# Five split-weight buffers at five byte offsets, and three matmul orders in the up projection

## The chip, the cores and the metric

The kernel runs on one core of one Trainium2 chip. The metric is device time in microseconds (us) for one execution of the whole program. The engines are named as in the profile: PE (TensorE, matmuls), PEld (its weight loads), DVE (VectorE), ACT (ScalarE), POOL (GpSimd) and SP (SyncE, which issues most DMAs). In a matmul, one operand is stationary (a 128 x 128 weight load ahead of the matmul) and the other is streamed through (up to 512 columns).

## The reference

One encoder block on 256 tokens with 2048 features, in float32. Cut to what matters here:

```
hn = rmsnorm(h, mix_norm_pre);  proj = hn @ w_in       # stages dtu, xbc, z
y  = [bidirectional SSD mixer, pooling mixer];  h += rmsnorm(y @ w_out)   # stage wo
hn = rmsnorm(h, ffn_norm_pre)
up = hn @ w_up                                          # stage up: 2048 x 11264
gate, val = split(up, 2)
ff = (gelu(dwconv(gate)) * val) @ w_down                # stage down (dn): 5632 x 2048
h += rmsnorm(ff)
gate = sigmoid(rmsnorm(h) @ w_gate)                     # stage gt
h += rmsnorm(gate * (p @ w_ple))                        # stage ple
```

## The kernel before

All large products are made at better than single-pass precision by splitting each operand into a high part (rounded to float32r) and a low part (the rest), and adding high x high, high x low and low x high. Weights come from HBM in float32 into one of three `raw` buffers. `split` (L142) then makes the two halves: ACT casts the high half (L154), DVE subtracts it from the raw weights to get the low half (L155). The halves lie in two tiles of 1056 float32r per partition, with the tags `whi` and `wlo`, of five buffers each, used in rotation. Each buffer has 4224 bytes in each partition. In the allocation of the program the five `whi` buffers, in the order in which they are used, start at bytes 42848, 59744, 55520, 51296 and 47072 of the partition, and the `wlo` buffers at 63968, 80864, 76640, 72416 and 68192. After them come 13 pages of 8192 bytes, from byte 85088 on, which hold activations and much else. Raw buffers lie ahead of the split buffers.

The kernel goes through its stages in the order of the reference. In all of them except xbc and up, activations are the stationary operand and the split weights are streamed. In xbc and up it is the other way round.

Up is the largest stage. Its output of 11264 features is cut into 11 slabs of 512 for the gate and 11 for the value, and each slab into two halves of 256 features (`i`), so that there are 44 blocks. A block takes 16 k-tiles of 128 input features; four k-tiles make a weight piece (128 x 1024), so that there are 176 pieces (`NPIECES`). `feature_pairs` (L384) issues the 16 matmuls of a piece: for each of four k-tiles and each of two groups of 128 features, the high half against a high-and-low pair of activations side by side (512 columns, `get.both(k)`), and then the low half against the high activations (256 columns), added onto the second half of the same accumulator:

```
mm(acc[f], wh[:, s], get.both(k), k == 0, False)
mm(acc[f][:, L:], wl[:, s], get(k)[0], False, k == NK - 1)
```

All matmuls are issued by the helper `mm`, so that the profile lists them under L90. The activations of up are in four pages (`wox`), with 2048 bytes for each k-tile. The main loop splits five pieces ahead (`next_part`), and after each piece one more, which is the piece five later. At the end of a block, `total` (L396) adds the two halves of each accumulator: ACT copies one (L399), DVE adds the other (L400). A pair of accumulators belongs to a block, and there are six such tiles, three pairs.

The order of ACT, DVE and SP in up is that in which the program lists the work (`in_order`). PE takes its matmuls in the order of the program.

In the names of the profile, numbers are left out: `ug_0h` is the high half of an even gate piece, `uv_1l` the low half of an odd value piece, `ga` and `va` the accumulators of gate and value, `dn...` those and the weights of down.

Of the kernel before, what the change touches and what calls it, by code (L numbers as in the profile page):

```python
# [12 lines left out]
F32R = mybir.dt.float32r  # L13
# [4 lines left out]
P = 128  # L18
L = 256
D = 2048  # L20
NK = D // P
# [32 lines left out]
def build(nc, a, out):  # L54
    x = a["x"][0]
# [5 lines left out]
    with tile.TileContext(nc) as tc, \  # L61
# [9 lines left out]
        def ins(r):  # L71
            return getattr(r, "ins", r)

        def page(name, dtype=F32):
            return gp.tile([P, 2048], dtype, tag="pg", bufs=13, name=name)
# [7 lines left out]
        def main(name):  # L83
            return [pm.tile([P, 512], F32, tag="main", name=f"{name}_{i}") for i in range(2)]
# [4 lines left out]
        def mm(o, lhsT, rhs, start, stop):  # L89
            last["pe"] = ins(nc.tensor.matmul(o, lhsT, rhs, start=start, stop=stop, skip_group_check=True))  # L90
# [15 lines left out]
        acc, acc2 = [main(f"dtu{t}") for t in range(2)], main("dtu2")  # L106
# [27 lines left out]
        low, among, four = small[:64, 592:593], small[:64, 593:597], small[:64, 597:601]  # L134
# [4 lines left out]

        spare, ready = {}, {}  # L140

        def split(name, src, nel, cuts=()):  # L142

            if name in ready:
                return ready.pop(name)
            if name in spare:
                hi, lo = spare.pop(name)
            else:
                hi = wp.tile([P, 1056], F32R, tag="whi", bufs=5, name=f"{name}h")
                lo = wp.tile([P, 1056], F32R, tag="wlo", bufs=5, name=f"{name}l")  # L150
            for c0, c1 in zip((0, *cuts), (*cuts, nel)):
                s = slice(c0, c1)
                if (name, c0) != ("dtu0", 0):
                    last["act"] = ins(nc.scalar.copy(hi[:, s], src[:, s]))  # L154
                last["dve"] = ins(nc.vector.tensor_sub(lo[:, s], src[:, s], hi[:, s].bitcast(F32)))  # L155
            return hi, lo
# [44 lines left out]
        @contextmanager  # L201
        def in_order():


            block = nc.cur_bb.bb.instructions
            seen = {i.name for i in block}
            yield
            for i in block:
                if i.name in seen or i.engine not in ORDERED:
                    continue  # L210
                if i.engine in chain:
                    tc.add_manual_dep(i, chain[i.engine].name,
                                      mybir.DependencyInfo(mybir.DependencyClass.NoSync, mybir.DependencyReason.DATA),
                                      reason="in_order")
                chain[i.engine] = i
# [58 lines left out]
        def seven_products(name, stage, w, k0, c0, a_, acc, alt, start, stop):  # L274

            if (stage, c0, k0) in sums_:
                r = raw(f"{name}r")
                last["dma"] = load(r[:, 512:], w[c0 // 1024, k0 // 2][:, 512:], not name.startswith(IN_ORDER))  # L280
                t, held = sums_[stage, c0, k0]
                if not held:
                    t = lp.tile([P, 2048], F32, tag="own", bufs=1, name=f"{name}t") if name == "gt18" else page(f"{name}t")
                    last["dma"] = load(t, sums_[stage, c0, k0][0], not name.startswith((*IN_ORDER, "gt18")))
            else:
                r = t = raw(f"{name}r", w[c0 // 1024, k0 // 2])
                if stage in APART:
                    t = page(f"{name}t")
                    add_blocks(r, t)
            b11 = split(f"{name}a", r[:, 512:1024], 512)  # L290
            b2 = split(f"{name}b", r[:, 1024:], 1024)
            if r is t:
                add_blocks(r)
            t42 = split(f"{name}d", t[:, 1024:], 1024)
            t31 = split(f"{name}c", t[:, :1024], 1024)

            for x, (wh, wl), c, o, own in (
                    ("a11", b11, 0, alt[0], True), ("a12", b2, 0, acc[0][0], False), ("a22", t42, 0, acc[1][0], False),
                    ("s4", b2, 512, acc[0][1], False), ("s2", t42, 512, alt[3], True), ("s1", t31, 512, alt[1], True),
                    ("s3", t31, 0, alt[2], True)):  # L300
                xh, xl = a_[x]
                for q, (xx, ww) in enumerate(((xh, wh), (xh, wl), (xl, wh))):
                    mm(o, xx, ww[:, c:c + 512], own and start and q == 0, own and stop and q == 2)
# [77 lines left out]
                                   k == 0 and q == 0 and f % 2 == 0, k == NK - 1 and q == 2)  # L381
                aside()

        def feature_pairs(n, part, get, acc):  # L384

            wh, wl = part
            for kk in range(4):
                k = 4 * n + kk  # L390
                for f in range(2):
                    s = slice(kk * 256 + f * P, kk * 256 + (f + 1) * P)
                    mm(acc[f], wh[:, s], get.both(k), k == 0, False)
                    mm(acc[f][:, L:], wl[:, s], get(k)[0], False, k == NK - 1)

        def total(o, acc):  # L396

# [79 lines left out]
                done = put(hn(k), x_part(k), vec(V_MIX + k))  # L477
            return done

        spare["dtu0"] = [wp.tile([P, 1056], F32R, tag=f"w{c}", bufs=5, name=f"dtu0{c[0]}") for c in ("hi", "lo")]  # L480
        turned = ins(nc.vector.tensor_copy(spare["dtu0"][0][:, :352], r0[:, :352]))
        with tc.issue_after(turned):
            front = x_panel(0, 1)
# [2 lines left out]
        for u in range(0, NK, 2):  # L486
            r = [wp.tile([P, 2048], F32, tag="raw", bufs=3, name=f"dtur{u}") if u else r0, page(f"dtur{u + 1}")]
            for j in range(2):
                k = u + j
# [17 lines left out]
            for j in range(2):  # L507
                k = u + j
                with tc.issue_after(front[0]), tc.issue_after(front[1]):
                    wh, wl = split(f"dtu{k}", r[j][:, :1056], 1056, ((352, 704), (704,), (352,))[k] if k < 3 else ())  # L510
# [234 lines left out]
        def job(f, *args):  # L745
            return lambda: f(*args)
# [83 lines left out]
        def gload(name, src):  # L830
            g = cp.tile([P, D], F32, tag="gain", name=name)
            load(g, src.partition_broadcast(P))
            return g
# [90 lines left out]
        h = [page(f"h{t}") for t in range(2)]  # L924
        for t in range(2):
            load(h[t], x[t * P:(t + 1) * P, :])
        hf = sublayer("wo", w_out, (list(range(8, 16)) + list(range(8)), [8,9,10,11,12,13,0,1,2,3,14,15,4,5,6,7]), cat, gload("gmix", a["mix_norm_post"][0]), h,
                      V_FN, Pairs, ((4,5),(2,3,4)), Sums("cs", cat))
# [42 lines left out]
        for i, w_ in enumerate(which[2:] + which[:2]):  # L971
            fetch, add, store = block_sums(*w_, i >= len(which) - 2)
            n = 45 * i // 10 + 4
# [62 lines left out]
        parts, slab = [], {}  # L1036

        def next_part():

            n = len(parts)  # L1040
            if n < NPIECES:
                s, v, i = blocks[n // 4]
                name = f"u{'gv'[v]}{s}{i}"
                if n % 2 == 0:
                    slab["raw"] = raw(f"{name}r{n // 2 % 2}", w_up[v, s, i, n // 2 % 2])
                parts.append(split(f"{name}{n // 2 % 2}_{n % 2}", slab["raw"][:, n % 2 * 1024:(n % 2 + 1) * 1024], 1024))
# [9 lines left out]
        def gate_norm(s, i):  # L1056
            v = slab[s][0][:, i * 512:(i + 1) * 512].rearrange("p (f t) -> p f t", f=2)
            nc.vector.tensor_tensor(v, v, slab["rfb"].unsqueeze(1).to_broadcast([P, 2, L]), op=ALU.mult)  # L1058
# [25 lines left out]
        with in_order():  # L1084
            for _ in range(5):
                next_part()
            for n in range(NPIECES):
                s, v, i = blocks[n // 4]
                if n % 4 == 0:
                    acc = main(f"{'gv'[v]}a{s}{i}")  # L1090
                with tc.issue_after(last["pe"]) if n in (6, 8) else nullcontext():
                    feature_pairs(n % 4, parts[n], hf, acc)
                if n % 4 == 3:
                    (value_out if v else gate_out)(s, i, acc)

                if n == 3:
                    row[0]()
                elif n == 5:
                    row[1]()
                next_part()  # L1100
                if n == 5:
                    row[2]()
                    gate_norm(0, 0)
                elif n in (6, 7):
                    (gelu if n == 7 else gate_conv)(0, 0)
                elif n >= 8 and n % 4 < 2 and blocks[n // 4 - 1][1] == 0:
                    (gelu if n % 4 else gate_conv)(blocks[n // 4 - 1][0], blocks[n // 4 - 1][2])
                for job in jobs_at[n]:
                    job()
# [114 lines left out]
        for half in range(2):  # L1224

            alt = [] if half else main(f"gts{half}")
            acc = [main(f"gt{half}{t}") for t in range(2)]
# [13 lines left out]
            for t in range(2):  # L1241
                for n, (o, c0) in enumerate(columns(acc[t])):
                    c1 = c0 + o.shape[-1]
                    c = slice(half * 1024 + c0, half * 1024 + c1)
# [102 lines left out]
```

## Time and profile before

| | |
|---|---|
| runs | 1109.44, 1109.47, 1108.57 us (median 1109.44) |
| span of the profiled execution, first to last instruction | 1106.4 us |
| its own time beside the span | not listed; the median lies 3.0 us above the span |
| granted TensorE clock, mean | 0.997 |
| PE busy | 1098.2 us, 99% |
| DVE busy | 978.2 us, 88% |
| ACT busy | 729.5 us, 66% |
| mean DMA rate | 327 GB/s |
| up on PE | from 289.1 to 783.9 us |

The busy time of PE counts each matmul from its start until its modelled end, and matmuls overlap in the pipeline (a 512-column matmul is listed with 0.39 us, but the next one starts after 0.23). So the pace of PE is read from one start to the next, and not from busy times.

### The profile page before, as it was taken

How to read it: one execution, taken by the hardware profiler on the slowest of the kernel's cores; microseconds unless marked ns; L12 is line 12 of the kernel's file. 1: busy time of each engine (PE TensorE's matmuls, PEld its weight loads, DVE VectorE, ACT ScalarE, POOL GpSimd, SP SyncE). 2: the span in 40 equal slices, each digit the busy share in tenths (PEclk: the TensorE clock that was granted, in tenths of full speed). 3: DMA queues.
4: the chain of work that ended last, by engine and by line, in shares of the span. 5: the costliest groups of instructions: out<-in, count | busy, mean ns of one | idle time of the engine just before them, and what ended most of it. 6: DMA issues, size and time to landing. Idle time of an engine off the chain costs nothing.

```text
span 1106.4 us, 16113 instructions
## 1 busy us (share of the span) xinstructions
PE 1098.2 (99%) x5946; PEld 947.8 (86%) x5946; DVE 978.2 (88%) x1372; ACT 729.5 (66%) x1067; POOL 86.2 (8%) x145
## 2 busy tenths in 40 slices
PE   9999999999999999999999999999999999999997
PEld 9999988888888888888888888888888888888886
DVE  6589998898868998889889988888999999999996
ACT  6958763556775565565756646657688878777773
POOL 0200000100100000000000000000000000051001
PEclk9999999999999999999999999999999999999998
DMA  9985358556589999989999998999999999995872
GB/s 366 364 336 187 111 191 346 209 211 231 182 356 400 400 403 349 394 350 367 386 359 373 369 394 335 405 356 421 357 408 370 376 346 388 414 384 220 315 270 76
DMA packets 57247, 361.71 MB, mean 327 GB/s; under 512 B 6352, under 2 KB 7504, under 8 KB 21200
## 3 DMA queue, kind: packets, MB, share of 16 engines
q1 hardware_dynamic: 45648, 298.71, 69.4%
q0 software_dynamic: 11088, 61.35, 14.4%
q8 instruction: 47, 0.77, 0.3%
q10 hardware_dynamic: 432, 0.62, 0.2%
q14 instruction: 32, 0.26, 0.1%
HBM read 306.65 MB, written 54.00 MB: 326 GB/s over the span
## 4 chain that ended last, share of the span: by engine, by line
PE 97%; ACT 1%; DVE 1%; issue 0%; POOL 0%; POOLq 0%
PE ga L90 22%; PE va L90 22%; PE dna L90 11%; PE woa L90 6%; PE xbc L90 5%; PE gt L90 5%; PE dns L90 4%; PE dtu L90 4%; PE z L90 4%; PE dn0s L90 2%; PE dn1s L90 2%; PE ple L90 1%; PE gts L90 1%; PE yd L90 1%; PE wos L90 1%; PE pw L90 1%
## 5 line engine op out<-in xcount | busy, mean ns | idle before, releaser
L90 PE MATMUL ga<-wox,ug_0h 128*128 128x512 f32 x352 | 125.5, 395 | 0.0
L90 PE MATMUL ga<-wox,ug_1h 128*128 128x512 f32 x352 | 125.2, 394 | 0.0
L90 PE MATMUL va<-wox,uv_0h 128*128 128x512 f32 x352 | 124.8, 393 | 0.0
L90 PE MATMUL va<-wox,uv_1h 128*128 128x512 f32 x352 | 124.8, 393 | 0.0
L90 PE MATMUL ga<-wox,ug_1l 128*128 128x256 f32 x352 | 99.1, 282 | 0.0
L90 PE MATMUL va<-wox,uv_0l 128*128 128x256 f32 x352 | 99.1, 281 | 0.0
L90 PE MATMUL va<-wox,uv_1l 128*128 128x256 f32 x352 | 99.1, 281 | 0.0
L90 PE MATMUL ga<-wox,ug_0l 128*128 128x256 f32 x352 | 99.1, 281 | 0.0
L272 DVE TENSOR_TENSOR dnb<-dnb 128x512 f32<-128x512 f32 x128 | 88.3, 690 | 3.0
L90 PEld LDWEIGHTS va<-wox,uv_0h 128*128 128x128 f32 x352 | 66.1, 188 | 15.0
L90 PEld LDWEIGHTS ga<-wox,ug_1h 128*128 128x128 f32 x352 | 66.1, 188 | 15.0
L90 PEld LDWEIGHTS va<-wox,uv_1h 128*128 128x128 f32 x352 | 66.1, 188 | 15.0
L90 PEld LDWEIGHTS ga<-wox,ug_0h 128*128 128x128 f32 x352 | 66.1, 188 | 14.8
L90 PEld LDWEIGHTS ga<-wox,ug_0l 128*128 128x128 f32 x352 | 66.2, 188 | 0.1
L90 PEld LDWEIGHTS ga<-wox,ug_1l 128*128 128x128 f32 x352 | 66.2, 188 | 0.0
L90 PEld LDWEIGHTS va<-wox,uv_0l 128*128 128x128 f32 x352 | 66.2, 188 | 0.0
L90 PEld LDWEIGHTS va<-wox,uv_1l 128*128 128x128 f32 x352 | 66.2, 188 | 0.0
L247 POOL DMA_DIRECT2D dns<-dnb x30 | 16.1, 536 | 321.8 <-DVE dnb L272 281.0
L843 ACT CAST he<-he 128x512 fp32r<-128x512 f32 x13 | 8.1, 621 | 41.9 <-DVE he L842 41.9
L985 ACT CAST hs<-hid 128x384 fp32r<-128x384 f32 (+1 forms) x44 | 23.4, 536 | 13.6 <-PE dna L90 13.3
L1065 ACT ACTIVATE fc<-gr,vt 128x256 f32<-128x256 f32 x44 | 26.1, 593 | 6.2 <-DVE gr L1058 6.1
L1136 POOL DMA_DIRECT2D hd<-hsum x24 | 12.9, 539 | 193.4 <-PE dn0s L90 83.1
(2491 smaller groups left out, 3300.4 us busy)
## 6 DMA issues: line engine op xcount, KB each, us to landing
dnb<-w_down SPq DMA_DIRECT2D x32, 1024.0 KB, 10.3
dns<-dnb POOLq DMA_DIRECT2D x30, 1024.0 KB, 6.8
hd<-hsum POOLq DMA_DIRECT2D x24, 512.0 KB, 8.3
zr<-w_z SPq DMA_DIRECT2D x8, 1024.0 KB, 4.9
dtur<-w_dtu SPq DMA_DIRECT2D x14, 528.0 KB, 8.5
hsum<-he POOLq DMA_DIRECT2D x13, 512.0 KB, 7.6
wo0r<-w_out_ SPq DMA_DIRECT2D x6, 1024.0 KB, 7.0
gtb<-w_gate SPq DMA_DIRECT2D x6, 1024.0 KB, 10.0
```

The source lines that it names most:

```text
L90: last["pe"] = ins(nc.tensor.matmul(o, lhsT, rhs, start=start, stop=stop, skip_group_check=True))
L247: nc.gpsimd.dma_start(t, pg[0])
L272: nc.vector.tensor_add(s[:, i], v[:, i], a[:, b])
L843: nc.scalar.copy(o[:, :512], s[:, :512])
L985: nc.scalar.copy(t[:, :c1], hid_part(k)[:, :c1])
L1065: nc.scalar.activation(c[:, f], v[:, f], AF.Identity, bias=vec(V_FCB + 4 * s + 2 * i + f), scale=vec(w + NF))
L1136: nc.gpsimd.dma_start(o.bitcast(F32), kept[k])
```

## The change

Instead of a `whi` and a `wlo` tile, each piece takes one tile which holds both halves, with a tag of its own for each of the five places in the rotation. The list `PLACES` gives each tile's size and where in it the high and the low half begin, in float32 elements. With the same start of the weights area as before, tiles laid out in the order of first use would begin at bytes 42848, 51424, 60000, 68608 and 77088, and the pages behind them at 85568. The halves then begin at these bytes modulo 256:

| place | 0 | 1 | 2 | 3 | 4 |
|---|---|---|---|---|---|
| high half, before | 96 | 96 | 224 | 96 | 224 |
| low half, before | 224 | 224 | 96 | 224 | 96 |
| high half, after | 96 | 224 | 0 | 32 | 64 |
| low half, after | 96 | 224 | 128 | 160 | 192 |
| pages, before / after | 96 / 64 | | | | |

In up, `feature_pairs` gets an order, which is the slab's number modulo 3: 0 is the order of before (one high, one low), 1 is two high and then two low, 2 is all eight high and then all eight low.

```diff
+        PLACES = ((2144, 0, 1088), (2144, 0, 1088), (2152, 40, 1096), (2120, 8, 1064), (2120, 8, 1064))
+        rotation = [0, 1, 2, 3, 4]
+
+        def weight_pair(name):
+            n = rotation.pop(0)
+            rotation.append(n)
+            size, h0, l0 = PLACES[n]
+            w = wp.tile([P, size], F32R, tag=f"w{n}", bufs=1, name=f"{name}w")
+            return w[:, h0:h0 + 1056], w[:, l0:l0 + 1056]
+
         def split(name, src, nel, cuts=()):
...
-                hi = wp.tile([P, 1056], F32R, tag="whi", bufs=5, name=f"{name}h")
-                lo = wp.tile([P, 1056], F32R, tag="wlo", bufs=5, name=f"{name}l")
+                hi, lo = weight_pair(name)
...
-        def feature_pairs(n, part, get, acc):
+        def feature_pairs(n, part, get, acc, order):
             wh, wl = part
-            for kk in range(4):
+
+            def high(kk, f):
                 k = 4 * n + kk
-                for f in range(2):
-                    s = slice(kk * 256 + f * P, kk * 256 + (f + 1) * P)
-                    mm(acc[f], wh[:, s], get.both(k), k == 0, False)
-                    mm(acc[f][:, L:], wl[:, s], get(k)[0], False, k == NK - 1)
+                mm(acc[f], wh[:, kk * 256 + f * P:kk * 256 + (f + 1) * P], get.both(k), k == 0, False)
+
+            def low(kk, f):
+                k = 4 * n + kk
+                mm(acc[f][:, L:], wl[:, kk * 256 + f * P:kk * 256 + (f + 1) * P], get(k)[0], False, k == NK - 1)
+
+            every = [(kk, f) for kk in range(4) for f in range(2)]
+            groups = ([(x,) for x in every], [every[i:i + 2] for i in range(0, 8, 2)], [every])[order]
+            for g in groups:
+                for x in g:
+                    high(*x)
+                for x in g:
+                    low(*x)
...
-        spare["dtu0"] = [wp.tile([P, 1056], F32R, tag=f"w{c}", bufs=5, name=f"dtu0{c[0]}") for c in ("hi", "lo")]
+        spare["dtu0"] = weight_pair("dtu0")
...
-                    feature_pairs(n % 4, parts[n], hf, acc)
+                    feature_pairs(n % 4, parts[n], hf, acc, s % 3)
```

## The prediction

> **What bounds the kernel now.** I read the page first (busy shares, the chain that ended last), then the time that PE spent waiting, then two stretches of the order of time on PE, down to single starts.
>
> ```profile
> PE 1098.2 (99%) x5946; PEld 947.8 (86%) x5946; DVE 978.2 (88%) x1372; ACT 729.5 (66%) x1067; POOL 86.2 (8%) x145
> ...
> PEclk9999999999999999999999999999999999999998
> ...
> PE 97%; ACT 1%; DVE 1%; issue 0%; POOL 0%; POOLq 0%
> PE ga L90 22%; PE va L90 22%; PE dna L90 11%; PE woa L90 6%; PE xbc L90 5%; PE gt L90 5%; PE dns L90 4%; PE dtu L90 4%; PE z L90 4%; PE dn0s L90 2%; PE dn1s L90 2%; PE ple L90 1%; PE gts L90 1%; PE yd L90 1%; PE wos L90 1%; PE pw L90 1%
> ```
>
> 97% of the chain is PE, at full granted clock; 44% of it is up (`ga`, `va`). What PE waited for in the whole span, and up against the neighbouring stretch:
>
> ```profile
> PE gof L90 <- ACT godg L1209: 1.9, 1, 1.9
> PE dtu L109 <- POOL ident masks.py:199: 1.4, 1, 1.4
> PE seg L90 <- ACT E L633: 0.2, 1, 0.2
> ```
>
> ```profile
> 289.10:783.90 494.80, 494.80 (x2846) 434.43 (x2846) 433.00 (x614) 303.64 (x460) 28.19 (x54) 1.00 0.95 370
> 784.00:1008.00 224.00, 224.00 (x975) 181.71 (x973) 214.26 (x255) 175.15 (x224) 30.52 (x33) 1.00 0.94 369
> ```
>
> PE waits 3.5 us in 1106.4 us, and none of it in up. So only the spacing of matmuls, start to start, can change the time; what ACT and DVE do matters only if they fall so far behind that PE starts to wait. Here are single starts in up. A weight piece is 16 matmuls, eight on the high half (512 columns) and eight on the low half (256); the rows kept are those at the start of six pieces, with two pairs inside the first.
>
> ```profile
> 451.50 0.39 PE L90 MATMUL va<-wox,uv_1h 128*128 128x512 f32 x1
> 451.72 0.28 PE L90 MATMUL va<-wox,uv_1l 128*128 128x256 f32 x1
> 451.84 0.40 PE L90 MATMUL va<-wox,uv_1h 128*128 128x512 f32 x1
> 452.08 0.28 PE L90 MATMUL va<-wox,uv_1l 128*128 128x256 f32 x1
> 452.20 0.40 PE L90 MATMUL va<-wox,uv_1h 128*128 128x512 f32 x1
> ...
> 454.31 0.39 PE L90 MATMUL va<-wox,uv_0h 128*128 128x512 f32 x1
> ...
> 457.09 0.39 PE L90 MATMUL va<-wox,uv_1h 128*128 128x512 f32 x1
> ...
> 459.90 0.39 PE L90 MATMUL va<-wox,uv_0h 128*128 128x512 f32 x1
> ...
> 462.68 0.39 PE L90 MATMUL va<-wox,uv_1h 128*128 128x512 f32 x1
> ...
> 465.46 0.39 PE L90 MATMUL va<-wox,uv_0h 128*128 128x512 f32 x1
> ```
>
> The pieces last 2.81, 2.78, 2.81, 2.78 and 2.78 us, 13.96 us for one turn through the five buffers: 2.792 on average (176 of them are 491.4 of the stage's 494.8 us). Nothing waits here, and the work is the same in all five; what differs is the buffer. In the program's allocation before, a 13-slot page of activations always starts at 96 mod 256, and the buffers of 4224 bytes alternate: in order of use the high half lies at 96, 96, 224, 96, 224 and the low half 128 bytes away from it. The two slow pieces are the two with the high half at 224. So address does count here, by 0.03 us or 1% of a piece. Measured from the page, the fast kind has its high half at 0 and its low half at 128, the slow kind 128 and 0.
>
> **The change, part by part.**
>
> *New offsets from the page.* The five new tiles take 480 bytes more than the ten old ones, so that the pages behind them move to 64 mod 256. Laid out in the order of first use, the pairs lie at (96, 96), (224, 224), (0, 128), (32, 160), (64, 192); from the page that is (32, 32), (160, 160), (192, 64), (224, 96), (0, 128). One of five is the fast kind of before. The other four use six offsets that up has not shown; the two known ones give 2.78 and 2.81, and I take their middle, 2.795, for each. A turn is then (2.78 + 4 x 2.795) / 5 = 2.792 us a piece: no change. The nearest rows for other offsets are in ple, where the stationary operand (`pth`, `ptl`, at 64) and the streamed buffers (96 and 224) are 96 or 224 apart, beside the same kind of matmul in down, where they are 0 or 128 apart:
>
> ```profile
> 283.87 0.39 PE L90 MATMUL ple<-ple_1h,ptl 128*128 128x512 f32 x1
> ...
> 285.48 0.39 PE L90 MATMUL ple<-ple_0h,pth 128*128 128x512 f32 x1
> ...
> 850.16 0.39 PE L90 MATMUL dn0s<-dn026dh,hd 128*128 128x512 f32 x1
> 850.38 0.39 PE L90 MATMUL dn0s<-dn026dl,hd 128*128 128x512 f32 x1
> 850.61 0.40 PE L90 MATMUL dn0s<-dn026dh,hd 128*128 128x512 f32 x1
> 850.85 0.39 PE L90 MATMUL dns<-dn026ch,hd 128*128 128x512 f32 x1
> ...
> 856.37 0.40 PE L90 MATMUL dn0s<-dn028ch,hd 128*128 128x512 f32 x1
> ```
>
> In ple there are 7 spacings in 1.61 us, 0.230 each; in down 27 in 6.21 us, 0.230 each. Single ones swing between 0.22 and 0.24 in down, and are steady in ple, but the mean is the same at both sets of offsets. This is my reason for the middle, and for 0 in all other stages, where the split buffers are streamed: 1,918 matmuls of 512 columns there. Bounds: in up, worst is every new pair at the longest pair above (451.84 to 452.20, 0.36), 2.88 a piece, (2.78 + 4 x 2.88) / 5 - 2.792 = 0.068, times 176 = +12.0 us; best is the shortest (451.50 to 451.84, 0.34), 2.72 a piece, -0.060 x 176 = -10.6 us. For the 1,918 others all at 0.22 or all at 0.24 would be 19 us either way; since the swing averages out in both rows, I keep 0.002 of it, 4 us either way.
>
> *Three orders.* Slabs 0, 3, 6, 9 keep high, low, high, low: 64 pieces. Slabs 1, 4, 7, 10 take two high, two low, and slabs 2, 5, 8 eight high, eight low: 112 pieces. The count of matmuls, weight loads and columns is the same; only neighbours change, from 512 beside 256 to 512 beside 512 and 256 beside 256. The first kind of run is down's 0.230. The second is xbc's, whose 24 rows from the first to the last of these hold 23 spacings:
>
> ```profile
> 60.64 0.28 PE L90 MATMUL xbc<-hnh,xb_1h 128*128 128x256 f32 x1
> ...
> 63.36 0.28 PE L90 MATMUL xbc<-hnh,xb_1l 128*128 128x256 f32 x1
> ```
>
> 2.72 / 23 = 0.1183 us. Eight of each are 8 x (0.230 + 0.1183) = 2.786 us, against 2.792 on average now: -0.006 x 112 = -0.7 us. Bounds: all of these pieces as the fast or the slow kind, -0.012 or +0.018 a piece, -1.3 or +2.0 us; this lies inside the bounds above.
>
> *One tile for both halves.* A buffer now comes free when both halves have been read. In up the last matmul of a piece is a low one in every order, so ACT's cast of a high half may start one low spacing, 0.12 us, later than before. Who feels it:
>
> ```profile
> 451.57 1.05 ACT L154 CAST uv_1h<-uv31r 128x1024 fp32r<-128x1024 f32 x1 [1.33 <-PE va L90]
> ```
>
> This cast starts when the piece before 451.50 has ended, and fills the buffer of the piece that starts at 462.68: 11.1 us of cover for 1.05 us on ACT and the subtraction on DVE behind it. Price 0. Queued behind that cast on ACT are the copies and convolution of the gate, with the same cover. In the other stages that split five at a time the high half is read last or one matmul apart, so the joint release comes with the high half's own: 0. In the first stage (dtu) the low product may follow by up to six matmuls; four pieces lie between: 0.
>
> *Reading out.* `total` reads f = 0 first. Its last matmul is now the last but one of a block in seven slabs (0.12 us before the end instead of 0.35), so ACT's copy starts 0.23 us later, 28 times. The accumulators are three deep (six tiles, two a block), so PE needs them again two blocks, or 22 us, later: 0. No DMA, queue or instruction is added; SP and POOL are not touched.
>
> **Sum:** 0 - 0.7 + 0 + 0 = -0.7 us. The profiled execution has a span of 1106.4 us, so 1105.7 after; the median of the runs shown, 1109.44, lies 3.0 us above the span, which I carry over: 1108.7 us.
>
> [...]
>
> **Rivals.**
>
> *Slower: the new offsets lock in the slow rhythm.* Place: the four new pairs in up, in any order. For it: a slow kind exists, holds through a whole piece, and the present layout has it in only two of five; single pairs reach 0.36. Against it: ple's offsets cost nothing. Price: all four at 2.81 is (2.78 + 4 x 2.81) / 5 - 2.792 = 0.012 x 176 = +2.1 us; at 2.88 it is +12.0. It decides when the four average over about 2.81. I put its middle at 1115 us.
>
> *Faster: the new offsets or the grouping avoid stalls.* For it: 0.34 and 0.22 occur, so neither 0.348 nor 0.230 is a floor. Against it: they never occur twice running. Price: all at the fast kind -2.1 us, at 2.72 -10.6; middle 1104 us.
>
> *The shared tile makes PE wait.* If a matmul on a high half had to wait for the DVE's write of the low half in the same tile, the price is up to about 1 us (the cast above takes 1.05) wherever a split is used at once; the first piece of dtu and a few units of down (DVE 214.26 of 224.00 us busy) are such places: +2 to +5 us, 1112 us. Against it: the low half is needed one matmul later anyway.
>
> **How the numbers follow.** About 2.2 us (0.2%) is what a measurement of this kernel can tell from no change. No change within that, around 1108.7: 0.44. Slower by offsets 0.25, by the shared tile 0.04: 0.29 together. Faster: 0.27. The time is that of the likeliest case, whose own range is 1107.2 to 1111.6. The full range takes in most of both rivals: half of the bounds of up below (-5.3) and two thirds above (+8.0): 1103 to 1117.
>
> **What would show it.** Right: pieces in up between 2.77 and 2.82 us in every order and buffer, PE still without a wait there, 512-column spacing in down at 0.230. Wrong: one offset whose pieces leave that band by several per cent, a slab order with its own level, a new line of PE waits on ACT or DVE, or a stage outside up that changes its spacing because its streamed buffers moved.

## The result and the profile after

The changed kernel took 1113.23 us (median of three, 1113.20 to 1114.55) against 1109.44 before: a ratio of 1.0042, with a 95% interval of 1.0027 to 1.0057. The ratio is estimated from all executions; the two medians alone give 1.0034. The kernel is slower by 0.4%, where 1108.7 and "no change" was forecast. The profiled execution took 1114.55 us, with a span of 1111.6 against 1106.4.

Busy times and chain, and what PE waited for (total in us, times, longest), from the page and the waits of the changed kernel:

```profile
PE 1103.6 (99%) x5946; PEld 948.7 (85%) x5946; DVE 978.7 (88%) x1372; ACT 728.8 (66%) x1067; POOL 84.2 (8%) x145
...
PE 97%; ACT 1%; DVE 1%; issue 0%; POOL 0%; POOLq 0%
```

```profile
PE gof L90 <- ACT godg L1226: 1.9, 1, 1.9
PE dtu L109 <- POOL ident masks.py:199: 1.4, 1, 1.4
PE seg L90 <- ACT E L650: 0.2, 1, 0.2
```

No wait has come, and none has grown: PE issues the same 5946 matmuls, and takes 5.2 us longer. So they stand further apart. By their starts, the last of which comes 5.4 us later, 1.6 us lie in up, 3.0 in the other stages from z on, and 0.8 ahead of z, where the profiles of the next five kernels also have 0.2 to 0.5 us more than before, those with the spacing of before included. Two stretches, one inside up and one inside down, count the matmuls. In these rows the first number behind the stretch is its length, the next are PE's busy time and its matmuls, then PEld, DVE, ACT, POOL, the granted clock, the DMA share and GB/s. First before, then after:

```profile
340.00:760.00 420.00, 420.00 (x2408) 368.63 (x2408) 369.45 (x522) 251.32 (x375) 24.45 (x46) 1.00 0.96 377
800.00:1000.00 200.00, 200.00 (x868) 162.35 (x867) 193.11 (x228) 158.06 (x198) 26.00 (x23) 1.00 0.96 379
```

```profile
340.00:760.00 420.00, 420.00 (x2402) 367.13 (x2401) 368.15 (x519) 247.41 (x372) 24.46 (x46) 1.00 0.96 375
800.00:1000.00 200.00, 200.00 (x862) 161.58 (x861) 191.86 (x226) 161.14 (x201) 26.33 (x24) 1.00 0.96 379
```

At the same clock, 6 matmuls fewer in 420 us of up (0.2%) and 6 fewer in 200 us of down (0.7%). Down loses more, though only up was given new orders. From the starts of all matmuls with 512 columns in both traces (outside up, two such in a row, without 28 that exceed 270 ns and one of 28 ns): 230.7 ns before and 232.3 after, 1,869 pairs in each; times 1,918 matmuls, this is 3.2 us. The table sorts them by offset: the byte address of the weights loaded meanwhile minus that of the operand that is streamed, modulo 256. The weights loaded meanwhile are those of the next matmul: in the kernel before, the load for the matmul at 850.38 us starts at 850.16, as the matmul ahead of it does; a load takes 188 ns. The changed kernel has these means:

| offset | 0 | 32 | 64 | 96 | 128 | 160 | 192 | 224 |
|---|---|---|---|---|---|---|---|---|
| ns, after | 230.8 | 233.3 | 232.0 | 234.1 | 232.1 | 233.5 | 230.6 | 231.6 |
| ns, before | 230.6 | | | | 230.7 | | | |

In up the order of time shows one row for a piece, since both halves have one name now. A place is the position of a piece's buffer in the rotation of five. These are pieces of a slab with the order of before (places 4, 0, 1, 2), of one with two and two (places 0, 1, 2), and of one with eight and eight (places 1, 2, 3); the start is the first number:

```profile
431.26 2.94 PE L90 MATMUL ga<-wox,ug_1w 128*128 128x512 f32 x16
434.04 2.94 PE L90 MATMUL ga<-wox,ug_0w 128*128 128x512 f32 x16
436.81 2.97 PE L90 MATMUL ga<-wox,ug_1w 128*128 128x512 f32 x16
439.62 2.87 PE L90 MATMUL ga<-wox,ug_0w 128*128 128x512 f32 x15
...
475.94 2.98 PE L90 MATMUL ga<-wox,ug_1w 128*128 128x512 f32 x16
478.75 2.98 PE L90 MATMUL ga<-wox,ug_0w 128*128 128x512 f32 x16
481.57 2.98 PE L90 MATMUL ga<-wox,ug_1w 128*128 128x512 f32 x16
...
520.84 2.99 PE L90 MATMUL ga<-wox,ug_1w 128*128 128x512 f32 x16
523.67 2.93 PE L90 MATMUL ga<-wox,ug_0w 128*128 128x512 f32 x16
526.44 2.96 PE L90 MATMUL ga<-wox,ug_1w 128*128 128x512 f32 x16
```

From one start to the next: 2.78, 2.77, 2.81 us, then 2.81 and 2.82, then 2.83 and 2.77. The medians over all pieces, in ns, by order (one high and one low in turn, two and two, eight and eight) and place:

| order, offsets (high, low) from the page | (32, 32) | (160, 160) | (192, 64) | (224, 96) | (0, 128) | mean |
|---|---|---|---|---|---|---|
| one, one | 2776 | 2807 | 2826 | 2774 | 2778 | 2792 |
| two, two | 2814 | 2822 | 2813 | 2777 | 2807 | 2807 |
| eight, eight | 2812 | 2832 | 2765 | 2801 | 2790 | 2800 |

Before, in the one order, the five places have 2775, 2776, 2816, 2777, 2816, which is 2792 on average. So up grew by 64 x 15 + 48 x 8 ns = 1.3 us by its orders. In the old order the new offsets leave the average where it was, 2792, though no longer each piece. (From the first to the last start the stage took 1.6 us more; the rest is in its first pieces.)

### The profile page after: what moved, and what is told of

Read it like the earlier page. It is cut to its first block, busy times and chain, and to the rows that moved or that the text cites. A ratio compares the mean times of both kernels' runs of the same rounds, so it can differ in the third digit from the quotient of the medians.

```text
span 1111.6 us, 16016 instructions
## 1 busy us (share of the span) xinstructions
PE 1103.6 (99%) x5946; PEld 948.7 (85%) x5946; DVE 978.7 (88%) x1372; ACT 728.8 (66%) x1067; POOL 84.2 (8%) x145
## 4 chain that ended last, share of the span: by engine, by line
PE 97%; ACT 1%; DVE 1%; issue 0%; POOL 0%; POOLq 0%
PE ga L90 22%; PE va L90 22%; PE dna L90 11%; PE woa L90 6%; PE xbc L90 5%; PE gt L90 5%; PE dns L90 4%; PE dtu L90 4%; PE z L90 4%; PE dn0s L90 2%; PE dn1s L90 2%; PE ple L90 1%; PE gts L90 1%; PE wos L90 1%; PE yd L90 1%; PE pw L90 1%
## 5 line engine op out<-in xcount | busy, mean ns | idle before, releaser
L90 PE MATMUL ga<-wox,ug_0w 128*128 128x512 f32 (+1 forms) x704 | 132.0, 338 | 0.0
L90 PE MATMUL ga<-wox,ug_1w 128*128 128x512 f32 (+1 forms) x704 | 131.3, 338 | 0.0
L90 PE MATMUL va<-wox,uv_1w 128*128 128x512 f32 (+1 forms) x704 | 130.4, 337 | 0.0
L90 PE MATMUL va<-wox,uv_0w 128*128 128x512 f32 (+1 forms) x704 | 130.3, 337 | 0.0
L90 PEld LDWEIGHTS ga<-wox,ug_0w 128*128 128x128 f32 x704 | 109.8, 188 | 15.6 <-ACT pl L933 0.2
L90 PEld LDWEIGHTS ga<-wox,ug_1w 128*128 128x128 f32 x704 | 109.7, 188 | 15.5
L90 PEld LDWEIGHTS va<-wox,uv_1w 128*128 128x128 f32 x704 | 109.7, 188 | 15.5
L90 PEld LDWEIGHTS va<-wox,uv_0w 128*128 128x128 f32 x704 | 109.7, 188 | 15.5
L90 PE MATMUL xbc<-hnh,xb_0w 128*128 128x256 f32 x192 | 37.7, 283 | 0.0
L90 PE MATMUL xbc<-hnh,xb_1w 128*128 128x256 f32 x192 | 37.1, 282 | 0.0
```

## The experiments

Every kernel was timed beside the kernel before; ratios are to it, with 95% intervals. Offsets are modulo 256.

### The parts alone

Only the places (the call in up passes order 0):

```diff
-                    feature_pairs(n % 4, parts[n], hf, acc, s % 3)
+                    feature_pairs(n % 4, parts[n], hf, acc, 0)
```

> The five new places, with the order of before (high, low, high, low) in all slabs of up. Theory A (the streamed buffers' offsets from the page cost time outside up, and the grouping costs time in up): in the changed kernel the slabs that kept this order averaged 2792 ns a piece, as before, so up stays within 0.5 us; outside up 512-column matmuls stay at 232.3 ns against 230.7 before, 1,918 of them: +3.2 us, about 1112.6. Theory B (the grouping alone is the cause): 1109.4. Theory C (the tile shared by both halves makes someone wait): about 1113, with the loss in waits and not in spacing.

Measured 1111.79 against 1108.53 us, ratio 1.0029 (1.0017 to 1.0040). Its rows for the two stretches:

```profile
340.00:760.00 420.00, 420.00 (x2409) 367.56 (x2408) 369.53 (x521) 250.18 (x374) 24.47 (x46) 1.00 0.96 377
800.00:1000.00 200.00, 200.00 (x862) 161.53 (x861) 191.63 (x226) 159.33 (x199) 26.40 (x24) 1.00 0.96 379
```

Up is back at 2409 matmuls; down has the 862 of the changed kernel. So the offsets cost 3.3 us (1111.79 - 1108.53), and all but 0.2 of it outside up.

Only the orders (the ten tiles of before, `whi` and `wlo`):

```diff
-            w = wp.tile([P, size], F32R, tag=f"w{n}", bufs=1, name=f"{name}w")
-            return w[:, h0:h0 + 1056], w[:, l0:l0 + 1056]
+            hi = wp.tile([P, 1056], F32R, tag="whi", bufs=5, name=f"{name}h")
+            lo = wp.tile([P, 1056], F32R, tag="wlo", bufs=5, name=f"{name}l")
+            return hi, lo
```

> The ten buffers of before, with three orders by slab. Theory A: outside up nothing changes (230.7 ns); in up the grouped slabs rise from 2792 to about 2800 to 2807 ns a piece (the averages of these slabs in the changed kernel), 112 pieces: +0.9 to +1.7 us, 1110.3 to 1111.1. Theory B: the whole loss, about 1113. Theory C: 1109.4.

Measured 1111.07 us, ratio 1.0022 (1.0013 to 1.0032).

```profile
340.00:760.00 420.00, 420.00 (x2400) 368.17 (x2399) 368.22 (x520) 248.66 (x374) 24.46 (x46) 1.00 0.96 375
800.00:1000.00 200.00, 199.94 (x865) 161.48 (x864) 192.53 (x227) 159.05 (x200) 17.77 (x24) 1.00 0.97 381
```

Up loses 8 matmuls in 420 us: its grouped slabs average 2805 (two and two) and 2808 (eight and eight), 64 x 13 + 48 x 16 ns = 1.6 us. Spacing outside up is as before, 230.7 ns. The profiled execution has 0.9 us more in down, in eight late starts. These are not spacing: weight loads waited there for DVE, 0.2 to 0.5 us each, the first of them for a low half that DVE had only just written:

```profile
860.30 0.19 PEld L90 LDWEIGHTS dna<-dn030bl,hs 128*128 128x128 f32 x1 [0.46 <-DVE dn030bl L159]
```

The changed kernel has no such wait in this part of down; a later kernel, the one that takes its lead-in from the map, has 0.9 us of late starts there too. Whether the orders brought these waits about is not shown. Both parts cost, and theory B, the orders alone, has fallen.

One tile, old offsets and order:

```diff
-        PLACES = ((2144, 0, 1088), (2144, 0, 1088), (2152, 40, 1096), (2120, 8, 1064), (2120, 8, 1064))
+        PLACES = ((2112, 0, 1056), (2112, 0, 1056), (2112, 1056, 0), (2112, 0, 1056), (2112, 1056, 0))
```

> One tile for both halves as in the changed kernel, but the halves at the offsets of before (high at 96, 96, 224, 96, 224, low 128 away, pages at 96), and the order of before. Theory A: spacing as before everywhere, pieces of 2776 and 2816 ns in the same rhythm, 1109.4. Theory B: 1109.4. Theory C: about 1113, with new waits of PE or ACT.

Measured 1108.54 us, ratio 1.0002 (0.9993 to 1.0011), with PE's three waits as they were. The pieces in up have the levels of before to 1 ns. Sharing a tile costs nothing that shows; theory C has fallen. With 3.3 us for the places and 1.3 for the orders, 4.6 us are accounted for; from the 1108.53 of 20 executions of the kernel before to 1113.23 it is 4.7.

### Is it the offset?

The kernel before with 32 bytes more between buffers and pages:

```diff
         spare["dtu0"] = [wp.tile([P, 1056], F32R, tag=f"w{c}", bufs=5, name=f"dtu0{c[0]}") for c in ("hi", "lo")]
+        nc.gpsimd.memset(wp.tile([P, 8], F32, name="pad"), 0.0)
```

> The kernel of before with 32 unused bytes (cleared once by POOL) between the split buffers and the pages, so that every offset between a buffer and a page is an odd multiple of 32 where it was 0 or 128. Theory A: streamed matmuls of 512 columns rise to about 233.4 ns (the classes 32 and 160 of the changed kernel), 1,918 x 2.7 = +5.2 us; in up the pieces with offsets (224, 96) are at 2774, the others (96, 224) unknown, between 2774 and 2816: up between -3 and 0 us. Together 1111.6 to 1114.6. Theories B and C: 1109.4, since neither order nor tiles change.

Measured 1113.14 us, ratio 1.0041 (1.0028 to 1.0053):

```profile
340.00:760.00 420.00, 420.00 (x2407) 367.85 (x2406) 369.94 (x522) 249.87 (x373) 24.68 (x47) 1.00 0.96 377
800.00:1000.00 200.00, 200.00 (x859) 161.09 (x858) 191.25 (x226) 159.41 (x200) 26.29 (x24) 1.00 0.95 376
```

32 unused bytes cost as much as the whole change: 859 matmuls in down instead of 868, at 233.1 ns. In up, the three places with the same offsets (224, 96) run at 2795, 2773 and 2795 ns; one pair of offsets, two levels. This was the first sign against single offsets as the cause.

The same 32 bytes ahead of the buffers, so that buffers and pages move together (the added line stands ahead of `hn = Panel("hn")`):

> The kernel of before with the 32 unused bytes ahead of the split buffers, so that buffers and pages move together by 32 bytes and their offsets from each other stay 0 and 128. If only the offset between the two counts: pieces of 2776 and 2816 ns and 230.7 ns outside up, as before. If the place itself modulo 256 counts: new levels, up to 5 us more, as with the 32 bytes between them.

One run: 1109.87 us, with these rows:

```profile
340.00:760.00 420.00, 420.00 (x2409) 368.66 (x2408) 369.46 (x522) 250.78 (x375) 24.53 (x46) 1.00 0.96 376
800.00:1000.00 200.00, 200.00 (x868) 162.41 (x867) 193.12 (x228) 158.34 (x199) 26.23 (x24) 1.00 0.96 379
```

Pieces take 2775, 2776, 2816, 2777, 2816 ns and matmuls outside up 230.6, as before, with 868 in down. So a move of both areas by 32 bytes changed nothing here, where 32 bytes of offset between them did (859 in down).

### Single offsets, or a rhythm?

In these kernels `weight_pair` gives tiles of 2112 elements at 96 and pages at 96; dtu has its halves at 0 and 1056, and all other pieces have theirs by `PLACES` (starts of the high and the low half in elements):

```diff
+            w = wp.tile([P, 2112], F32R, tag=f"w{n}", bufs=1, name=f"{name}w")
+            if name.startswith("dtu"):
+                return w[:, :1056], w[:, 1056:]
+            h0, l0 = PLACES[n]
+            return w[:, h0:h0 + 1024], w[:, l0:l0 + 1024]
```

The first has `PLACES = ((0, 1040),) * 5` and order 2 throughout.

> All five pieces outside dtu with the high half at 0 and the low half at 64 from the page (one tile, pages at 96), and in all slabs of up eight high and then eight low. Theory A with additive spacings (a matmul's spacing goes by the offset between what it streams and the weights loaded meanwhile): in the changed kernel's grouped slabs a 512-column matmul over weights at 0 took 228.2 ns, a 256-column one over weights at 64 took 114.4 ns, so a piece is 8 x 342.6 = 2741 ns against 2792 before: -9.0 us in up; outside up the streamed classes are 0 and 192, 230.7 ns, no change: 1099.5. Rival (a spacing hangs on the rhythm that a whole sequence settles into, not on single offsets): pieces between 2765 and 2800, 1104 to 1110.

Measured 1108.94 us, ratio 0.9998 (0.9990 to 1.0007). Each piece takes 2780 ns, not 2741. The theory that a spacing belongs to an offset has fallen; its rival holds. In the changed kernel the 228.2 and 114.4 ns had been seen in pieces with other partners, in its eight-and-eight slabs; in its two-and-two slabs the same offsets have 233.1 and 117.2.

All at the fast kind of before, `((0, 1056),) * 5`, order 0:

> All five pieces at the fast kind of before (high 0, low 128 from the page), order of before. Theory A: 2776 ns a piece instead of 2792: -2.8 us, and outside up 230.7 ns as before: 1105.7. If the fast kind is fast only between slow ones: 1108.5.

Measured 1105.55 against 1108.85 us, ratio 0.9970 (0.9959 to 0.9981); 2773 ns in every piece, as expected. It is faster than both kernels. Outside up the mean is as before, 230.8 ns, but its two offsets part: 229.9 at 0 and 232.5 at 128, where the kernel before has 230.6 and 230.7. So the table by offset above holds for its own sequences only.

A map, `((0, 1040), (16, 1088), (24, 1072), (32, 1080), (16, 1056))`, three orders:

> A map for up: the pairs (high, low) at (0, 64), (64, 0), (96, 192), (128, 224), (64, 128) from the page in the five places, three orders by slab. Additive spacings: in eight-and-eight order (0, 64) takes 2741 ns, (64, 0) and the others as their single offsets make it, the same in each pair that shares an offset (64 twice). Rhythm: pairs that share an offset differ by over 20 ns a piece.

One run, 1111.41 us. In the order of time, pieces of the places 0 to 3 in a slab with the order of before:

```profile
432.97 2.94 PE L90 MATMUL ga<-wox,ug_0w 128*128 128x512 f32 x16
435.74 2.88 PE L90 MATMUL ga<-wox,ug_1w 128*128 128x512 f32 x16
438.46 2.96 PE L90 MATMUL ga<-wox,ug_0w 128*128 128x512 f32 x16
441.26 2.93 PE L90 MATMUL ga<-wox,ug_1w 128*128 128x512 f32 x16
```

The second, with (64, 0), takes 2.72 us; inside it, pairs of 227 and 113 ns follow each other without change. All other cells lie at 2772 to 2830. In the eight-and-eight order (0, 64) takes 2784 here, so again not 2741.

Then (64, 0) in all five places, `((16, 1088),) * 5`, order 0, first everywhere and then in up alone:

```diff
+            h0, l0 = (PLACES if name[0] == "u" or not OTHER else OTHER)[n]
```

`OTHER` is empty in the first and holds the offsets of before, `((0, 1056), (0, 1056), (1056, 0), (0, 1056), (1056, 0))`, in the second.

> All five pieces outside dtu with the high half at 64 and the low half at 0 from the page, one high and one low in turn. The rhythm theory, with what the map showed for this pair in this order (pairs of 227 and 113 ns, 2723 a piece, the same in all 13 pieces seen): up gains 69 ns x 176 = 12.1 us; outside up the streamed classes are 192 and 0, 231.5 ns as in the run that had these (+0.8 ns x 1,918 = +1.6 us): 1098 to 1099. If the pair is fast only among its neighbours in the map: pieces of 2770 to 2800, about 1108.

> The same in up alone; all other stages but dtu have their halves at the offsets of before. Rhythm theory: up gains the same 12.1 us, outside up spacing stays at 230.7 ns: 1096.5 to 1097.5. If offsets outside up do not matter: the same as the run with them everywhere.

Measured 1116.70 (1112.26 to 1117.26), ratio 1.0072 (1.0059 to 1.0084), and 1110.32, ratio 1.0003 (0.9982 to 1.0024; it leaves out the two longest executions, and one very short one pulls it down; the medians alone give 1.0016). Both expectations were missed by over 12 us. Both kernels have levels: of five executions of the first, one took 1112.26 and four 1116.55 to 1117.26; of twelve of the second, nine took 1109.44 to 1111.22, two 1114.23 and 1114.93, and one, as short as expected, 1097.26. The profiled execution of the second (1111.22):

```profile
432.69 2.96 PE L90 MATMUL ga<-wox,ug_0w 128*128 128x512 f32 x16
435.49 2.96 PE L90 MATMUL ga<-wox,ug_1w 128*128 128x512 f32 x16
438.29 2.96 PE L90 MATMUL ga<-wox,ug_0w 128*128 128x512 f32 x16
```

2.80 us a piece, from the eighth piece to the last. The same 16 matmuls at the same offsets take 2.72 us in the map and 2.80 here.

A second map in up, `((8, 1088), (24, 1088), (1040, 8), (1048, 8), (1072, 32))`, order 0, others as before:

> A second map for up, in the order of before: (32, 0), (96, 0), (64, 32), (96, 32), (192, 128) from the page in the five places; elsewhere the offsets of before. If the rhythm of (64, 0) comes from the low half lying 64 bytes behind the high half, (96, 32) and (192, 128) reach about 2723 as well and the other three do not. If it comes from the streamed operand meeting the low half at 0, (32, 0) and (96, 0) are near it and (96, 32) and (192, 128) are not.

One run, 1109.68 us: 2808, 2776, 2783, 2817, 2777 ns. Neither guess about (64, 0) is borne out.

### What sets the rhythm

The map differed in what ran ahead of (64, 0). Two kernels put one or two (0, 64) pieces into each turn, the rest (64, 0), in up alone: `((0, 1040), (16, 1088), (16, 1088), (16, 1088), (16, 1088))`, and the same with the third place at `(0, 1040)`.

> Of the five places in up the first at (0, 64), the other four at (64, 0); elsewhere the offsets of before; order of before. Theory (the spacing is that of a rhythm into which a sequence falls, and what precedes decides which): after a (0, 64) piece the map always fell into 227 and 113 ns. Then four pieces of about 2723 and one of about 2773 in each turn: 2733 against 2792, -10.4 us, 1098, in all executions. Rival (the fast rhythm needs the whole sequence of the map, or chance): pieces at 2800 after some turns, and executions that differ by several us: about 1110.

> As before, with two of the five at (0, 64): (0, 64), (64, 0), (0, 64), (64, 0), (64, 0). Theory: each (64, 0) piece at 2723, each (0, 64) at about 2773: 2743 on average, -8.6 us, 1100, and the same in all executions. Rival: about 1110 with a spread.

Measured ratios 1.0006 (0.9998 to 1.0015) and 0.9993 (0.9982 to 1.0005); (0, 64) at 2773 and (64, 0) at 2800 in both profiled executions, and one execution of the second, of twelve, at 1100.70 us. Early in up the first of these two kernels shows a third level: its eighth to tenth piece, all (64, 0), take 2827, 2827 and 2826 ns. Kept for the remaining 169 pieces, 27 ns more would be an estimated 4.6 us, which is about what the longer executions of the two kernels with (64, 0) in all places have over the others; none of those was profiled, so this is not shown.

The theory as I had put it, that the piece ahead decides by its offsets, has fallen. But a (0, 64) piece alternates between pairs of 228 and 118 and of 231 and 116 or 117. In the map it ends on a pair of 230 or 231 and 115 or 116, and the fast piece follows; in these two kernels it ends on 229 and 117 or 228 and 117 or 118, and the slow piece follows. By the starts in the traces this holds at every such change in up from the eighth piece on: 10 in the map (in slabs with the order of before), 33 and 67 in these two. That left the phase, the kind of pair on which the piece ahead ends.

So the last two take the lead-in from the map as it is. One uses the map's five places for the first 12 pieces of up, and (64, 0) from then on:

```diff
+            if name[0] == "u":
+                counted.append(name)
+            h0, l0 = OTHER[n] if name[0] != "u" else PLACES[n] if len(counted) <= 12 else PLACES[1]
```

The other has (0, 64), three times (64, 0), and the map's (64, 128) as the fifth in each turn.

> Up in the order of before; the first 12 pieces have the five pairs of the first map, in which (64, 0) always ran at 227 and 113 ns; all later pieces have (64, 0). Elsewhere the offsets of before. Theory (a sequence keeps the rhythm in which it starts, and the boundary decides which): pieces from the 13th on stay at 2723 ns, 69 x 164 = 11.3 us less, about 1097.5, in nearly all executions. Rival (the fast rhythm does not last without its neighbours, or the start falls differently each time): 2800 from some piece on, or executions that differ by up to 13 us.

> In each turn of five (0, 64), three times (64, 0), and (64, 128); elsewhere the offsets of before. Theory (the end of the piece ahead decides): if (64, 128) leaves (0, 64) in the same phase as in the map, (64, 0) runs at 2723 and a turn averages (2773 + 3 x 2723 + 2805) / 5 = 2749 ns against 2792: -7.6 us, 1101. If not, 2800 for the three, 2796 on average: 1109.

Measured 1096.92 us (1096.65 to 1097.98) against 1108.71, ratio 0.9893 (0.9878 to 0.9908), and 1101.29, ratio 0.9934 (0.9921 to 0.9946), both as expected. The order of time of the first, where the rhythm begins and near the end of up, and its two stretches:

```profile
321.30 2.94 PE L90 MATMUL va<-wox,uv_0w 128*128 128x512 f32 x16
324.07 2.88 PE L90 MATMUL va<-wox,uv_1w 128*128 128x512 f32 x16
326.79 2.88 PE L90 MATMUL va<-wox,uv_0w 128*128 128x512 f32 x16
...
740.23 2.88 PE L90 MATMUL ga<-wox,ug_0w 128*128 128x512 f32 x16
742.95 2.88 PE L90 MATMUL ga<-wox,ug_1w 128*128 128x512 f32 x16
745.67 2.88 PE L90 MATMUL ga<-wox,ug_0w 128*128 128x512 f32 x16
```

```profile
340.00:760.00 420.00, 420.00 (x2473) 372.12 (x2472) 378.35 (x534) 255.28 (x389) 25.58 (x48) 1.00 0.97 386
800.00:1000.00 200.00, 200.00 (x870) 161.70 (x869) 192.01 (x227) 157.06 (x202) 17.61 (x29) 1.00 0.93 370
```

From the twelfth piece to the last, 2.72 us each: 2473 matmuls in the stretch of up instead of 2408. In the second kernel, too, all 33 (0, 64) pieces from the eighth piece on that are followed by (64, 0) end on 230 or 231 and 115 or 116, and the fast piece follows. The first is the fastest kernel of the study, with the matmuls of before in their old order; only addresses differ.

## Why the prediction was wrong, and where it was right

*What bounds the kernel* was right: no wait came, and everything that moved was PE's spacing.

*The term for other stages, 0, is the step that failed.* It measured 3.2 to 3.3 us (1,918 matmuls at 232.3 instead of 230.7 ns; the places alone: 1.0029). The working rested on the claim that "the mean is the same at both sets of offsets", taken from 7 spacings of ple at 0.230. These are a steady stretch. Over all of ple in the same trace, 40 spacings, the means are 233.2 ns at 96 and 232.0 at 224, and the rows just ahead of the quoted ones show single spacings of 0.24. Seven from a row of forty were no mean. The places alone, the orders alone and the two kernels with 32 bytes more show what stood in its place: in these runs spacing outside up went with the offset between buffers and pages, 230.7 ns at the offsets of before, 232.3 at the new ones, 233.1 with 32 bytes between and 230.6 with the same bytes ahead. The bounds of 4 us either way did hold the true value.

*The term for the orders, -0.7 us,* had the wrong sign: +1.3 us in the changed kernel and +1.6 with the old offsets. It priced both new orders as eight and eight; two and two, which it left without a row of its own, makes up 1.0 of the 1.3 us. It put together a piece from down's 0.230 and xbc's 0.118, but in up eight and eight over (0, 128) take 2790 ns against 2773 to 2778 in turn. The spacings of other stages' sequences did not carry over. The bounds, -1.3 to +2.0, held.

*The new offsets in up, 0,* came out at 2792 a piece, the number forecast, though from levels of 2774 to 2826 and not from a common middle: the number is right by luck.

*One tile, reading out:* 0, as the kernel with one tile shows (1.0002).

*The rivals:* the slower one was the right sign, but it was placed in up; its cost came mostly from the other stages (3.2 to 3.3 us). The shared tile is refuted. The faster one exists, but is not reached by this change. (Its 0.348 is an eighth of a piece of 2.78 us.) Its 0.34, on which the lower bound of -10.6 us rests too, was read from rounded times: by starts in ns that pair has 345, and in up of the kernel before no pair from the 13th piece on is under it. That a pair of 0.340 exists after all was luck. The objection, that such pairs "never occur twice running", holds for the kernel before alone; the kernel with the lead-in runs 0.340 for 164 pieces. The range, 1103 to 1117, held the time. (The likeliest case's own range, 1107.2 to 1111.6, is 2.2 us about the time before, 1109.4, and not about 1108.7.)

Open: why the offset counts. The runs show that 32 bytes of offset between buffers and pages moved the spacing outside up from 230.7 to 233.1 ns; whether it is the weight load that takes the time, they do not show. They also show that what ran ahead decided between two lasting rhythms, 2720 and 2800 ns a piece; that it does so through the phase fits all 143 changes in four traces, but the phase alone was never varied. Against a part of ACT or DVE in it speaks that pieces keep their length to 1 ns over 164 pieces while those two work (255.28 and 378.35 of 420 us in the kernel with the lead-in); no run tests it. Smaller steps were not tried, nor whether 256 bytes is the right period. Also open is why one execution in twelve of two kernels was shorter by 13 and 7 us: the length fits the fast rhythm, but neither was profiled.

## What to carry to other kernels

Where PE never waits, look at the starts of its matmuls, sorted by buffer: a level that repeated with the rotation of the buffers was a matter of addresses here, and addresses were worth 1% (1096.9 against 1108.7 us). 32 bytes of padding between the streamed and the stationary operands moved their offset, and cost 0.4% here with no other trace than the spacing; the same padding ahead of both did nothing (one run). So hold the offset fixed when something else is to be measured. Do not price a spacing from a short stretch or another stage's sequence; count over hundreds, and repeat executions: twelve of one kernel lay between 1097.26 and 1114.93 us here.

## What the runs showed of the hardware that was not expected

Sequences of matmuls kept the rhythm that they had taken up: the same 16 instructions over the same offsets took 2720 or 2800 ns (3%), for 164 and 168 pieces without one exception in two profiled executions. What ran ahead decided which, as the lead-in of 12 pieces shows (1096.92 against 1110.32 us); at all 143 changes from (0, 64) to (64, 0) that were counted it went with the last pair of the piece ahead. Single spacings were not additive: 228.2 and 114.4 ns, each seen in one mixture, gave 2780 ns a piece together where their sum is 2741.
